# A hybrid decoder layer on one core: weight sums placed one unit before their split, both retention pairs in the other product order, one copy per value tile, later transposes and an earlier split

## The chip, the cores and the metric

One core of a Trainium2 chip runs the whole layer in one launch. The time is the device time of that launch in microseconds, as the median of several executions. The profile is taken of one further execution; its span is the time from the first to the last instruction that the profile shows.

## The reference

One layer on 512 tokens of width 1024, in float32. What is computed, cut to the lines that matter:

```python
h = rmsnorm(x, g_mix);  z = h @ w_in        # 9728 columns: retention q,k,v,gate; 3 attention groups; merge gates
y = retention_chunkwise(rq, rk, rv)          # 4 heads, chunks of 128
ret_branch = (silu(rg) * rmsnorm(y)) @ w_ret_out
for g, (window, dilation) in enumerate(((128, 1), (512, 4), (2048, 16))):
    o_g, lse_g = dilated_window_attention(aq[:, :, g], ak[:, :, g], av[:, :, g], window, dilation)
att_branch = (sum over g of softmax(lse)[g] * o_g) @ w_att_out
x = x + (gate_r * ret_branch + gate_a * att_branch) @ w_o
x = x + square(relu(rmsnorm(x, g_mlp) @ w_up)) @ w_down          # inner width 4096
return x + sigmoid(rmsnorm(x, g_ple) @ w_ple_gate) * (p @ w_ple_proj)
```

## The kernel before

**Three passes.** Every float32 product is made of three passes on PE (the tensor engine): the high part of one factor by the high part of the other, and two cross terms (`mm3`, lines 262 to 264). So each weight tile must be split in two. A weight unit is 256 rows by 512 columns, 512 KB. SP issues its load into a tile `raw` (`fetch`, line 212), ACT copies it, rounded, into `whi` (line 250), and DVE subtracts to get `wlo` (line 251). `units` keeps the splits two units ahead of PE, three in the last part (`AHEAD`). The pool has six `raw` tiles and four pairs of split tiles.

**Seven products.** Most large products are written as seven products of blocks in place of eight (`seven_products`). Product m takes one factor of the weights: B11, B21 and B22 are blocks as they are loaded; T1, T2, T3 and T4 are sums of blocks. Each is two units (0 and 1). For products that name T1 in `vector`, T1's sum is one DVE instruction of 128x1024 (line 226), which adds the raw tile of B11 into the raw tile of T1. It is written into the program right after the split of the unit in whose place `added` holds it: B11's own. The other sums come from DMAs on the queue of POOL which add in flight (lines 214 and 228).

The order of the products is a table of (product, half). With `SEVEN` the weight units run B11_0, T1_0, B11_1, T1_1, B21_0, and so on; with `HALVES` they run B11_0, B11_1, T1_0, T1_1, B21_0, ... `HALVES` is used for w_up and w_down (four products of each), `SEVEN` for the values of attention groups 1 and 2 and for the retention pairs (values and gates together, two products).

**Order on the engines.** A scheduler orders the instructions of ACT, DVE and PE except in stretches under `manual_schedule` (first attention part, w_o, and from the last w_down on), where ACT and DVE run in the order in which the code is written. What is put off runs through `later(lag, fn)`: `fn` runs after so many ticks, a tick being one panel of matmuls.

**The attention places.** `values_seven` evaluates the values of groups 1 and 2; products 6 and 7 give a tile `m` of 128 tokens, which SP copies into the strided value tile `v` with four DMAs of 32x512 each (line 764). `scores` has the exponentials `se` of a group turned by PE (`pe`, line 694) some ticks after the softmax. `rescale` makes the last merge factors: DVE f (line 863), ACT's exponential of f (864), DVE w, st, inv, f (866 to 871), ACT scales the sixteen blocks of `se` by inv (876), DVE copies f into `wide` (878), and PE transposes wide into `pc` (884).

**w_up.** `up_products` squares the rectified result, forms sums of it, and splits them as left factors of w_down. What is put into `before` runs inside the following w_down product at the index given; the split for product 2 stands at indexes 0 and 5 there (line 1340).

Of the kernel before, what the change touches and what calls it, by code (L numbers as in the profile page):

```python
# [17 lines left out]
P = 128  # L18
# [9 lines left out]
DIL = 4  # L28
# [47 lines left out]
def R(ap):  # L76
    return ap.bitcast(F32R)


class Block:  # L80
# [90 lines left out]
    def plan_seven(self, w, r0, c1, c2, order, vector=()):  # L171

        cols = (c1, c2)
        q = lambda i, j, u: w[r0 + 512 * i + 256 * u : r0 + 512 * i + 256 * (u + 1), cols[j] : cols[j] + 512]
        n = len(self.plan)
        units = [(FACTOR[m], v) for m, u in order for v in ((0, 1) if u is None else (u,))]
        at = lambda name, u: n + units.index((name, u))
        for name, u in units:
            if name == "T1":
                src = q(0, 1, u) if name in vector else (q(0, 1, u), q(0, 0, u))  # L180
                if name in vector:
                    self.added[at("B11", u)] = at("T1", u), at("B11", u)
            elif name == "T4" and name in vector:
                self.added[max(at("B21", u), at("T2", u))] = at("T2", u), at("B21", u)
                src = (None, at("T2", u))
            elif name[0] == "B":
                src = q(int(name[1]) - 1, int(name[2]) - 1, u)
            else:
                prev, ij = {"T2": ("T1", (1, 1)), "T3": ("B22", (0, 1)), "T4": ("T2", (1, 0))}[name]
                k = at(prev, u)  # L190
                self.chained[k] = q(*ij, u)
                src = (None, k)
            self.plan.append((src, None))
# [538 lines left out]
    def values_seven(self, scale, ready=None):  # L732

        nc = self.nc
        for j in range(2):
            self.force(("S", j))
        held, out = {}, {}

        def tile(n):
            if n not in out:  # L740
                out[n] = self.big("v")
            return out[n]

        def after(m, p, ps):
            t = p if m in (1, 2, 3, 6) else 2 + p
            main = m in (1, 2, 4)
            r = scale[0 if main else 1]
            by = {} if r is None else dict(scale=r[:, t : t + 1])
            if main:
                o = tile(0)[:, t]  # L750
            elif m in (3, 5):
                o = self.tmp("m3") if m == 3 else self.tabp.tile([P, 512], F32, tag="tab", name=self.nm("m5"))
                held[{3: 6, 5: 7}[m], p] = o
            else:
                o = held.pop((m, p))
            if m in (1, 3, 5, 4):
                nc.scalar.activation(o, ps, AF.Copy, **by)
            elif r is None:
                nc.vector.tensor_tensor(o, o, ps, op=ALU.add)
            else:  # L760
                nc.vector.scalar_tensor_tensor(o, ps, r[:, t : t + 1], o, op0=ALU.mult, op1=ALU.add)
            if m in (6, 7):
                for q in range(DIL):
                    nc.sync.dma_start(tile(1)[32 * t : 32 * (t + 1), q], o[q : P : DIL])
            if m in (2, 4) and ready is not None:
                ready(t, o)

        self.seven_products(self.left, after)
        return tile(0), tile(1)

    def scores(self, g, qT, kT, rq, past, held=None, lag=2):

        nc = self.nc
# [5 lines left out]
        def block(r):  # L779
# [17 lines left out]
                    hs = slice(2 * hp, 2 * hp + 2)  # L797
                    es.append(self.softmax(sc, 256, 2, self.mask[:, 0:256], rq[:, r, hs], m[:, hs], l[:, hs]))
            for e in es:
                self.later((5, 8, 11)[g], lambda e=e: turn(e, r), ("pT", g, r))  # L800

        def turn(e, r):
            if g == 2:
# [209 lines left out]
    def retention(self, dec, kd):  # L1013
# [8 lines left out]
        for pr in range(2):  # L1022
# [19 lines left out]
                    nc.scalar.activation(s, g, AF.Sigmoid, scale=r)  # L1042
                    nc.vector.scalar_tensor_tensor(g, g, r, s, op0=ALU.mult, op1=ALU.mult)

            self.seven_products(left, after)
            A.append(self.big("A"))
            for hh in range(2):
                self.ret_head(2 * pr + hh, (qT, kT, kd), tile("v"), tile("G"), inner, eps, A)
# [259 lines left out]
    def up_products(self, h2):  # L1308

        nc = self.nc  # L1310
        U, split = self.slots()
        held, before = {}, {}
        v = lambda ap: ap.rearrange("p (k t) -> p k t", k=2)

        def after(m, p, ps):
# [10 lines left out]
                nc.scalar.activation(x, x, AF.Relu, scale=1.0 if m == 2 else -1.0)  # L1326
            nc.scalar.activation(x, x, AF.Square)
            a11, a12, a21 = held.get((3, p)), held[1, p], held[5, p]
            if m == 6:
                split(1, v(a11), k)  # L1330
            elif m == 7:
                nc.vector.tensor_tensor(a11, a11, a21, op=ALU.subtract)
            elif m == 4:
                nc.vector.tensor_tensor(a21, x, a21, op=ALU.subtract)
                split(5, v(a21), k)
                self.differ(a21, x, a11)
                s3 = self.tmp("r3")
                rest = lambda m, a: lambda: split(m, v(a), k)
                third = lambda: self.differ(s3, a12, a21)
                for i, fn in ((p, third), (5 * p, rest(2, a12)), (1 + p, rest(3, s3)), (4 + p, rest(6, a21)),  # L1340
                              (7 + p, rest(7, a11)), (9 + p, rest(4, x))):
                    before.setdefault(i, []).append(fn)

        self.seven_products(lambda m, kk: (R(h2[m][:, 0, kk]), R(h2[m][:, 1, kk])), after, HALVES, "cb")
        return U, before


# [109 lines left out]
    def make_plan(self):  # L1457
# [7 lines left out]
        for c in range(2):  # L1465
            self.plan_cols(w, RQ + 256 * c, KD)
        for c in (0, 512):
            self.plan_seven(w, 0, RV + c, RG + c, SEVEN, ("T1", "T4"))
        self.plan_mix()
        self.plan_seven(a["w_o"][0], 0, 512, 0, SEVEN)  # L1470
        for half in range(2):
# [45 lines left out]
```

## Time and profile before

| what | us |
|---|---|
| median of 3 runs (lowest, highest) | 954.35 (953.08, 955.14) |
| the profiled execution, its own time | 955.36 |
| its span | 953.6 |
| PE busy | 943.3 |
| DVE busy | 718.4 |
| ACT busy | 562.1 |
| mean granted clock of PE, as a share of full speed | 0.997 |

The profiled execution took 1.01 us more than the median, and 1.8 us more than its span, which lies before the first and after the last instruction shown. PE's share of the span is 99%: a change gains either by making PE do less, or by closing the few places where it waits or runs at a lower clock. DVE and ACT are busy for 75% and 59% of the span; what they do counts only where PE waits for it.

### The profile page before, as it was taken

What the parts mean: (1) busy time and instruction counts of PE and PEld (TensorE: products, weight loads), DVE (VectorE), ACT (ScalarE), POOL (GpSimd) and SP (SyncE); (2) the same over time, 40 slices, a digit from 0 to 9 for tenths busy, and PEclk for the clock granted to TensorE, in tenths of its full rate; (3) what the DMA queues carried; (4) which work ended last, traced back from release to release, by engine and by line L of the source; (5) the groups of instructions that cost most, each with busy time, mean ns of one, the idle gap of its engine ahead of it and who ended that gap; (6) DMA issues with size and microseconds to landing.
All of it is one profiled execution on the core that took longest, in us unless ns stands there. A gap on an engine that the chain in (4) does not pass through costs nothing.

```text
span 953.6 us, 14325 instructions
## 1 busy us (share of the span) xinstructions
PE 943.3 (99%) x5357; PEld 826.2 (87%) x5357; DVE 718.4 (75%) x997; ACT 562.1 (59%) x1065; POOL 159.5 (17%) x140
## 2 busy tenths in 40 slices
PE   9999999999899999999999999999999999999998
PEld 6888888888788888999988888988998998998887
DVE  7789964766697849386937889799499689769953
ACT  5657775445745566576714446884494486467651
POOL 0322210222001112223012211111212302112100
PEclk9999999999999999999999999999999999999999
DMA  9953466258437645869737677868958968876911
GB/s 333 282 170 82 106 141 215 64 118 195 148 111 155 173 100 138 163 181 217 232 115 236 148 178 214 206 153 222 199 156 202 191 183 157 224 172 159 288 50 56
DMA packets 92549, 162.87 MB, mean 171 GB/s; under 512 B 8608, under 2 KB 20544, under 8 KB 92480
## 3 DMA queue, kind: packets, MB, share of 16 engines
q1 hardware_dynamic: 65168, 113.37, 36.4%
q0 software_dynamic: 23936, 46.14, 29.0%
q10 hardware_dynamic: 3376, 2.44, 0.9%
q8 instruction: 42, 0.69, 0.3%
q14 instruction: 27, 0.22, 0.1%
HBM read 153.49 MB, written 6.34 MB: 168 GB/s over the span
## 4 chain that ended last, share of the span: by engine, by line
PE 92%; DVE 3%; ACT 1%; issue 1%; DMA 1%; POOL 1%; SPq 0%; ACTq 0%; POOLq 0%; DVEq 0%
PE pg L264 25%; PE pg L262 25%; PE pg L263 25%; PE pa L264 3%; PE pa L263 3%; PE pa L262 3%; PE po L835 1%; PE ph L590 1%; DVE wlo L251 1%; PE pe L694 1%; PE sc L787 1%; PE ry L1083 1%; PE kv L1070 1%; PE ry L1085 1%; DVE ro L578 0%
## 5 line engine op out<-in xcount | busy, mean ns | idle before, releaser
L251 DVE TENSOR_TENSOR wlo<-raw,whi 128x1024 fp32r<-128x1024 f32 (+1 forms) x258 | 306.8, 1198 | 112.7 <-ACT whi L250 111.8
L250 ACT ACTIVATE whi<-raw 128x1024 fp32r<-128x1024 f32 (+1 forms) x257 | 266.3, 1041 | 212.1 <-PE pg L264 87.2
L263 PE MATMUL pg<-f,whi 128*128 128x256 f32 x384 | 108.7, 283 | 0.0
L264 PE MATMUL pg<-f,wlo 128*128 128x256 f32 x384 | 108.7, 283 | 0.0
L262 PE MATMUL pg<-f,whi 128*128 128x256 f32 x384 | 108.7, 283 | 0.0
L262 PE MATMUL pg<-whi,hh 128*128 128x512 f32 x248 | 98.6, 398 | 0.0
L264 PE MATMUL pg<-whi,hl 128*128 128x512 f32 x248 | 97.1, 392 | 0.0
L263 PE MATMUL pg<-wlo,hh 128*128 128x512 f32 x248 | 96.8, 390 | 0.0
L262 PE MATMUL pg<-whi,f 128*128 128x512 f32 x192 | 75.4, 393 | 0.0
L263 PE MATMUL pg<-wlo,f 128*128 128x512 f32 x192 | 74.8, 389 | 0.0
L264 PE MATMUL pg<-whi,f 128*128 128x512 f32 x192 | 74.8, 389 | 0.0
L262 PEld LDWEIGHTS pg<-f,whi 128*128 128x128 f32 x384 | 73.7, 192 | 0.2
L263 PEld LDWEIGHTS pg<-f,whi 128*128 128x128 f32 x384 | 73.7, 192 | 0.2
L264 PEld LDWEIGHTS pg<-f,wlo 128*128 128x128 f32 x384 | 73.7, 192 | 0.0
L228 POOL DMA_DIRECT2D raw<-in_w_in x32 | 38.9, 1216 | 197.8 <-DVE wlo L251 193.0
L264 PEld LDWEIGHTS pg<-whi,hl 128*128 128x128 f32 x248 | 46.6, 188 | 9.8
L263 PEld LDWEIGHTS pg<-wlo,hh 128*128 128x128 f32 x248 | 46.6, 188 | 9.2
L262 PEld LDWEIGHTS pg<-whi,hh 128*128 128x128 f32 x248 | 46.6, 188 | 9.2
L228 POOL DMA_DIRECT2D raw<-in_w_down x24 | 29.0, 1215 | 139.3 <-DVE wlo L251 108.2
L262 PE MATMUL pg<-whi,us 128*128 128x512 f32 x128 | 52.1, 407 | 0.0
L228 POOL DMA_DIRECT2D raw<-in_w_up x24 | 29.0, 1211 | 135.0 <-DVE wlo L251 124.7
L264 PE MATMUL pg<-whi,us 128*128 128x512 f32 x128 | 50.0, 391 | 0.0
(280 smaller groups left out, 2298.0 us busy)
## 6 DMA issues: line engine op xcount, KB each, us to landing
raw<-in_w_in SPq DMA_DIRECT2D x72, 512.0 KB, 4.1
raw<-in_w_in POOLq DMA_DIRECT2D x32, 512.0 KB, 6.2
raw<-in_w_up SPq DMA_DIRECT2D x32, 512.0 KB, 4.6
raw<-in_w_down SPq DMA_DIRECT2D x32, 512.0 KB, 4.6
raw<-in_w_up POOLq DMA_DIRECT2D x24, 512.0 KB, 6.6
raw<-in_w_down POOLq DMA_DIRECT2D x24, 512.0 KB, 5.9
x<-in_x SPq DMA_DIRECT2D x8, 512.0 KB, 8.2
raw<-in_w_ret_out SPq DMA_DIRECT2D x8, 512.0 KB, 3.8
```

Source lines behind the costliest of these rows:

```text
L228: self.nc.gpsimd.dma_start(raw, self.chained[i].rearrange("(k p) n -> p k n", p=P), accum_op=ALU.add)
L250: self.pin(nc.scalar.activation(R(hi[:, i]), raw[:, i], AF.Copy))
L251: nc.vector.tensor_tensor(R(lo[:, i]), raw[:, i], hi[:, i], op=ALU.subtract)
L262: t.matmul(ps, sh, mh, start=first, stop=False, skip_group_check=more)
L263: t.matmul(ps, sh, ml, start=False, stop=False, skip_group_check=more)
L264: t.matmul(ps, sl, mh, start=False, stop=last, skip_group_check=more)
L590: self.nc.tensor.transpose(ps[:, t * P : (t + 1) * P], rots[t][:, h * HD : (h + 1) * HD], self.ident)
L694: self.nc.tensor.transpose(ps[:, k * P : (k + 1) * P], e[:, k * P : (k + 1) * P], self.ident)
L787: nc.tensor.matmul(sc[:, h * P : (h + 1) * P], qT[:, h, rs], kT[:, h, rs], start=True, stop=True)
L835: nc.tensor.matmul(po[:, h * P : (h + 1) * P], v[:, vt, h * HD : (h + 1) * HD], pt, start=b == 0, stop=b == len(blocks) - 1)
L1070: nc.tensor.matmul(ps, kd[:, n, hs], v[:, n, c], start=True, stop=True)
L1083: nc.tensor.matmul(y, sT[0][:, r], v[:, i, c], start=True, stop=i == 0)
```

## The change

There are five edits.

1. In `plan_seven` T1's sum on DVE is put behind the split of the unit just before T1's own, in place of behind B11's. With `SEVEN` these are the same place; with `HALVES` the sum is written one unit later.
2. In `values_seven` one DMA of 32x4x512 (256 KB) takes the place of four of 32x512 (64 KB), for each of eight value tiles.
3. In `scores` the transposes of group 2's exponentials are put off by 15 ticks in place of 11.
4. The two retention pairs use `HALVES` in place of `SEVEN`, in the plan of the loads and in the products.
5. In `up_products` the split for product 2, for both halves p, runs at index 11 of the same w_up product (before its last unit), in place of at indexes 0 and 5 of the w_down product behind it.

```diff
--- before.py
+++ after.py
@@ -179,7 +179,7 @@
             if name == "T1":
                 src = q(0, 1, u) if name in vector else (q(0, 1, u), q(0, 0, u))
                 if name in vector:
-                    self.added[at("B11", u)] = at("T1", u), at("B11", u)
+                    self.added[at("T1", u) - 1] = at("T1", u), at("B11", u)
             elif name == "T4" and name in vector:
                 self.added[max(at("B21", u), at("T2", u))] = at("T2", u), at("B21", u)
                 src = (None, at("T2", u))
@@ -760,8 +760,7 @@
             else:
                 nc.vector.scalar_tensor_tensor(o, ps, r[:, t : t + 1], o, op0=ALU.mult, op1=ALU.add)
             if m in (6, 7):
-                for q in range(DIL):
-                    nc.sync.dma_start(tile(1)[32 * t : 32 * (t + 1), q], o[q : P : DIL])
+                nc.sync.dma_start(tile(1)[32 * t : 32 * (t + 1)], o)
             if m in (2, 4) and ready is not None:
                 ready(t, o)
 
@@ -797,7 +796,7 @@
                     hs = slice(2 * hp, 2 * hp + 2)
                     es.append(self.softmax(sc, 256, 2, self.mask[:, 0:256], rq[:, r, hs], m[:, hs], l[:, hs]))
             for e in es:
-                self.later((5, 8, 11)[g], lambda e=e: turn(e, r), ("pT", g, r))
+                self.later((5, 8, 15)[g], lambda e=e: turn(e, r), ("pT", g, r))
 
         def turn(e, r):
             if g == 2:
@@ -1042,7 +1041,7 @@
                     nc.scalar.activation(s, g, AF.Sigmoid, scale=r)
                     nc.vector.scalar_tensor_tensor(g, g, r, s, op0=ALU.mult, op1=ALU.mult)
 
-            self.seven_products(left, after)
+            self.seven_products(left, after, HALVES)
             A.append(self.big("A"))
             for hh in range(2):
                 self.ret_head(2 * pr + hh, (qT, kT, kd), tile("v"), tile("G"), inner, eps, A)
@@ -1309,7 +1308,7 @@
 
         nc = self.nc
         U, split = self.slots()
-        held, before = {}, {}
+        held, before, own = {}, {}, {}
         v = lambda ap: ap.rearrange("p (k t) -> p k t", k=2)
 
         def after(m, p, ps):
@@ -1326,7 +1325,9 @@
                 nc.scalar.activation(x, x, AF.Relu, scale=1.0 if m == 2 else -1.0)
             nc.scalar.activation(x, x, AF.Square)
             a11, a12, a21 = held.get((3, p)), held[1, p], held[5, p]
-            if m == 6:
+            if m == 2:
+                own.setdefault(11, []).append(lambda: split(2, v(x), k))
+            elif m == 6:
                 split(1, v(a11), k)
             elif m == 7:
                 nc.vector.tensor_tensor(a11, a11, a21, op=ALU.subtract)
@@ -1337,11 +1338,11 @@
                 s3 = self.tmp("r3")
                 rest = lambda m, a: lambda: split(m, v(a), k)
                 third = lambda: self.differ(s3, a12, a21)
-                for i, fn in ((p, third), (5 * p, rest(2, a12)), (1 + p, rest(3, s3)), (4 + p, rest(6, a21)),
+                for i, fn in ((p, third), (1 + p, rest(3, s3)), (4 + p, rest(6, a21)),
                               (7 + p, rest(7, a11)), (9 + p, rest(4, x))):
                     before.setdefault(i, []).append(fn)
 
-        self.seven_products(lambda m, kk: (R(h2[m][:, 0, kk]), R(h2[m][:, 1, kk])), after, HALVES, "cb")
+        self.seven_products(lambda m, kk: (R(h2[m][:, 0, kk]), R(h2[m][:, 1, kk])), after, HALVES, "cb", own)
         return U, before
 
 
@@ -1465,7 +1466,7 @@
         for c in range(2):
             self.plan_cols(w, RQ + 256 * c, KD)
         for c in (0, 512):
-            self.plan_seven(w, 0, RV + c, RG + c, SEVEN, ("T1", "T4"))
+            self.plan_seven(w, 0, RV + c, RG + c, HALVES, ("T1", "T4"))
         self.plan_mix()
         self.plan_seven(a["w_o"][0], 0, 512, 0, SEVEN)
         for half in range(2):
```

What this makes of the order, at three places. First DVE around the last merge factors of the attention (f to wide), with the retention's first T1 sum (`raw<-raw,raw`); before:

```order
L251 TENSOR_TENSOR wlo_2564<-raw_2561,whi_2563 128x1024
L863 TENSOR_TENSOR f_2484<-st_2159,st_1123 128x16
L226 TENSOR_TENSOR raw_2755<-raw_2755,raw_2749 128x1024
L866 TENSOR_TENSOR w_2487<-f_2484,st_1123 128x16
L867 TENSOR_TENSOR st_2159<-st_2159,w_2487 128x4x4
L870 RECIPROCAL inv_2490<-st_2159 128x16
L871 TENSOR_TENSOR f_2484<-f_2484,inv_2490 128x16
L878 COPY wide_2509<-f_2484 128x4x4
```

and now:

```order
L251 TENSOR_TENSOR wlo_2540<-raw_2537,whi_2539 128x1024
L862 TENSOR_TENSOR f_2463<-st_2147,st_1123 128x16
L865 TENSOR_TENSOR w_2466<-f_2463,st_1123 128x16
L866 TENSOR_TENSOR st_2147<-st_2147,w_2466 128x4x4
L869 RECIPROCAL inv_2469<-st_2147 128x16
L870 TENSOR_TENSOR f_2463<-f_2463,inv_2469 128x16
L877 COPY wide_2488<-f_2463 128x4x4
L226 TENSOR_TENSOR raw_2719<-raw_2719,raw_2707 128x1024
```

The sum has moved from behind f to behind wide. Second PE behind the transpose of wide (`pc`), at the start of the retention's query columns; `pe` are the transposes of the exponentials `se`. Before:

```order
L884 MATMUL pc_2551<-ident,wide_2509 16x128
L264 MATMUL pg_2179<-whi_2463,hl_148 128x512
L694 MATMUL pe_2598<-ident,se_2356 128x128 x2
L262 MATMUL pg_2616<-hh_145,whi_2557 128x512
L694 MATMUL pe_2598<-ident,se_2356 128x128 x2
L263 MATMUL pg_2616<-hl_147,whi_2557 128x512
L694 MATMUL pe_2605<-ident,se_2372 128x128
L264 MATMUL pg_2616<-hh_145,wlo_2558 128x512
L694 MATMUL pe_2605<-ident,se_2372 128x128
L262 MATMUL pg_2616<-hh_145,whi_2557 128x512
L694 MATMUL pe_2605<-ident,se_2372 128x128 x2
```

and now:

```order
L883 MATMUL pc_2527<-ident,wide_2488 16x128
L264 MATMUL pg_2167<-whi_2445,hl_148 128x512
L262 MATMUL pg_2578<-hh_145,whi_2533 128x512
L263 MATMUL pg_2578<-hl_147,whi_2533 128x512
L264 MATMUL pg_2578<-hh_145,wlo_2534 128x512
L262 MATMUL pg_2578<-hh_145,whi_2533 128x512
```

with the first `pe` of this group 24 matmuls of the query columns later:

```order
L263 MATMUL pg_2578<-hl_148,whi_2539 128x512
L264 MATMUL pg_2578<-hh_146,wlo_2540 128x512
L694 MATMUL pe_2633<-ident,se_2344 128x128 x4
L694 MATMUL pe_2640<-ident,se_2360 128x128 x4
L262 MATMUL pg_2579<-hh_145,whi_2533 128x512
```

The transposes, which stood between the first matmuls behind pc, follow the whole of the first unit's product. Third DVE in the last w_down, around the split of its two T1 units (`wlo` of the raw tiles that the sum writes); before:

```order
L251 TENSOR_TENSOR wlo_8448<-raw_8362,whi_8447 128x1024
L1301 TENSOR_TENSOR f_8400<-r_8090,f_8400 128x512
L251 TENSOR_TENSOR wlo_8453<-raw_8369,whi_8452 128x1024
L1306 SCALAR_TENSOR_TENSOR r_8090<-r_8429,r_8185 128x512
L1301 TENSOR_TENSOR f_8471<-r_8404,f_8471 128x512
L1306 SCALAR_TENSOR_TENSOR r_8436<-r_8025,r_8090 128x512
L251 TENSOR_TENSOR wlo_8478<-raw_8475,whi_8477 128x1024
```

and now:

```order
L251 TENSOR_TENSOR wlo_8423<-raw_8347,whi_8422 128x1024
L1300 TENSOR_TENSOR f_8378<-r_8066,f_8378 128x512
L226 TENSOR_TENSOR raw_8426<-raw_8426,raw_8341 128x1024
L1305 SCALAR_TENSOR_TENSOR r_8066<-r_8407,r_8161 128x512
L251 TENSOR_TENSOR wlo_8431<-raw_8426,whi_8430 128x1024
L1300 TENSOR_TENSOR f_8449<-r_8382,f_8449 128x512
L1305 SCALAR_TENSOR_TENSOR r_8414<-r_8001,r_8066 128x512
L251 TENSOR_TENSOR wlo_8456<-raw_8453,whi_8455 128x1024
```

The sum of the second T1 unit, which stood in the w_up product ahead, is now the second instruction ahead of that unit's wlo, and ACT's whi of the same tile stands between the two.

## Rows read from the trace of the kernel before

**Rows 1.** The page, busy time of each engine over the span, and the chain of waits by engine

```profile
PE 943.3 (99%) x5357; PEld 826.2 (87%) x5357; DVE 718.4 (75%) x997; ACT 562.1 (59%) x1065; POOL 159.5 (17%) x140
...
PE 92%; DVE 3%; ACT 1%; issue 1%; DMA 1%; POOL 1%; SPq 0%; ACTq 0%; POOLq 0%; DVEq 0%
```

**Rows 2.** Waits of PE: line waited for, us in total, times, longest

```profile
PE pc L884 <- DVE wide L878: 3.0, 1, 3.0
```

**Rows 3.** Timeline of SP, 244 to 264 us: start, duration, engine, line, operation

```profile
246.87 7.26 SPq L764 DMA_DIRECT2D v<-m  x8
```

**Rows 4.** Timeline of all engines, 250 to 257 us

```profile
250.78 0.17 DVE L863 TENSOR_TENSOR f<-st,st 128x16 f32<-128x16 f32 x1
...
251.69 0.20 ACT L864 ACTIVATE f<-f 128x16 f32<-128x16 f32 x1
...
252.70 0.39 PE L263 MATMUL pg<-wlo,hh 128*128 128x512 f32 x1
253.73 1.22 DVE L226 TENSOR_TENSOR raw<-raw,raw 128x1024 f32<-128x1024 f32 x1 [2.79 <-DMA v<-m]
...
254.88 0.17 DVE L866 TENSOR_TENSOR w<-f,st 128x16 f32<-128x16 f32 x1
...
255.78 0.18 DVE L878 COPY wide<-f 128x16 f32<-128x16 f32 x1
...
256.11 0.37 PE L884 MATMUL pc<-ident,wide 128*16 128x128 f32 x1 [3.02 <-DVE wide L878]
```

**Rows 5.** Windows: busy us of each engine, granted clock, DMA share

```profile
core 0: us, PE busy (x) PEld busy (x) DVE busy (x) ACT busy (x) POOL busy (x), PEclk, DMA share, GB/s
108.00:112.00 4.00, 3.17 (x14) 2.36 (x13) 3.93 (x8) 2.69 (x11) 1.71 (x2) 1.00 0.73 109
252.00:256.00 4.00, 1.09 (x5) 0.56 (x3) 2.09 (x6) 1.14 (x5) 0.00 (x0) 0.99 0.26 77
256.00:260.00 4.00, 3.89 (x16) 3.09 (x17) 0.00 (x0) 4.00 (x15) 0.00 (x0) 0.59 0.64 244
260.00:264.00 4.00, 4.00 (x23) 3.35 (x22) 3.26 (x6) 3.98 (x11) 0.00 (x0) 1.00 0.10 35
```

**Rows 6.** Timeline of ACT, 250 to 262 us

```profile
255.63 4.79 ACT L876 ACTIVATE se<-se,inv 128x128 f32<-128x128 f32 x16 [2.86 <-DVE inv L870]
```

**Rows 7.** Every instruction of line 226 (ns min/median/max)

```profile
L226 DVE TENSOR_TENSOR raw<-raw,raw x32: 1214/1218/1227, 56.9 to 854.8; 128x1024 f32<-128x1024 f32 x32
```

**Rows 8.** Timeline of DVE in the last w_down

```profile
867.80 0.68 DVE L1301 TENSOR_TENSOR f<-r,f 128x512 fp32r<-128x512 f32 x1
868.40 1.22 DVE L251 TENSOR_TENSOR wlo<-raw,whi 128x1024 fp32r<-128x1024 f32 x1
...
877.45 1.22 DVE L251 TENSOR_TENSOR wlo<-raw,whi 128x1024 fp32r<-128x1024 f32 x1
```

**Rows 9.** Timeline of PE in the last w_down

```profile
870.89 0.39 PE L262 MATMUL pg<-whi,f 128*128 128x512 f32 x1
...
871.34 0.39 PE L264 MATMUL pg<-whi,f 128*128 128x512 f32 x1
...
879.45 0.39 PE L263 MATMUL pg<-wlo,f 128*128 128x512 f32 x1
```

**Rows 10.** Windows again, in the last w_down

```profile
866.00:870.00 4.00, 4.00 (x20) 3.30 (x19) 4.00 (x6) 2.88 (x4) 1.20 (x1) 1.00 0.00 0
```

**Rows 11.** Timeline, first w_down, the second T1 weight unit on ACT, DVE and PE

```profile
628.46 1.05 ACT L250 ACTIVATE whi<-raw 128x1024 fp32r<-128x1024 f32 x1
...
630.04 1.22 DVE L251 TENSOR_TENSOR wlo<-raw,whi 128x1024 fp32r<-128x1024 f32 x1
...
635.37 0.39 PE L262 MATMUL pg<-whi,f 128*128 128x512 f32 x1
```

**Rows 12.** DMA issues: kind, count, KB each, median us to landing

```profile
v<-m SPq DMA_DIRECT2D x32, 64.0 KB, 4.2
```

**Rows 13.** Timeline of PE, 256 to 275 us, the first product with group-two values

```profile
269.76 1.05 PE L835 MATMUL po<-pT,v 128*128 128x128 f32 x8
```

## The prediction

> **What bounds the kernel now.** I read the page first: PE is busy for 943.3 of 953.6 us and 92% of the chain that ended last is PE [rows 1]. None of the five edits takes a matmul away, so work saved on DVE, ACT or SP is worth nothing in itself; only a place where PE waits or runs slowly can give time. The waits of PE name one such place of any size: 3.0 us, once, for `wide` [rows 2]. The timeline there shows why [rows 4]. PE starts its last matmul at 252.70 and the transpose of wide at 256.11. DVE had f at 250.78 and ACT its exponential from 251.69 to 251.89, but DVE, in order, stood before w at the retention's first T1 sum. That could not start before its load had landed, behind SP's eight copies of value tiles [rows 3], ran from 253.73 for 1.22 us, and only then came w at 254.88 and wide at 255.78.
>
> The windows show a second cost [rows 5]. PE was busy for 1.09 us of 252 to 256; in the next 4 us the granted clock was 0.59 of full speed, a mixture of the two levels 1.2 and 2.4 GHz, and from 260 on it was 1.00. So that window lost 4.00 x (1 - 0.59) = 1.6 us. A shorter pause cost no clock: in 108 to 112 PE was idle for 0.83 us and the grant stayed at 1.00. Stall and clock together: 4.5 us.
>
> **Edits 1 and 4 at the attention's end: -2.9 and -1.6.** The order now has the sum behind wide. The chain from w to the end of wide took 255.96 - 254.88 = 1.08 us [rows 4]. Started after the exponential, at some 251.95, it ends at 253.03. The transpose followed wide's end by 0.15 us, which gives 253.18 in place of 256.11: 2.9 us gained, with 0.25 us of idle left behind the matmul that ended near 252.93. That is less than the 0.83 us that cost no clock, so I take the 1.6 us as gained too. Bounds: stall 0 (if something else holds w) to 3.0 (the whole wait); clock 0 to 1.6. The sum itself is late now: it runs when its load lands, as before at 253.73, and its split is needed only after the query columns, so it costs nothing there.
>
> [...]
>
> **Edit 3: 0.** The first eight transposes `pe` leave the first matmuls behind pc and come 24 and more matmuls later, by 24 x 0.23 = 5.5 us (matmul starts of rows 9 give the 0.23: two steps in 0.45). ACT's sixteen scalings of `se` take 4.79 us [rows 6]. They can begin with inv near 252.8, as the chain above moves by 2.9 us, and end near 257.6, ahead of the transposes at 253.2 + 5.5 = 258.7. Without this edit PE would follow the scalings closely. Behind the transposes the first product with group two's values is at 269.76 [rows 13], 11 us later, which covers the delay. Bounds: 0, and a wait of at most one scaling, 0.3 us (4.79/16).
>
> **Edit 2: 0.** SP issues 8 DMAs for 32; the old ones took 7.26/8 = 0.9 us each on its queue [rows 3], so some 22 us of SP's time go. A 64 KB copy landed 4.2 us after issue [rows 12]. The last landed before 256 and the first matmul that reads them is at 269.76 [rows 13]; 14 us of cover hold even if one large copy takes three times as long. The loads of `raw` behind them may land sooner, but edit 1 has taken the sum that waited there out of PE's way. Bounds: 0 and 0, with the cover gone at most 4.2 us.
>
> **Edit 1 in w_up and w_down: 0 but for the last.** A sum one unit later, with the split behind it, can delay a T1 unit by 1.22 [rows 7] and ACT's copy, 1.05. In the first w_down the second T1 unit has whi done at 629.51 and wlo at 631.26, and PE takes it at 635.37 [rows 11]: 4.1 us to spare against 2.3. The w_up products and the retention pairs are written the same way.
>
> **Edit 1 in the last w_down: +0.9.** There DVE and ACT run as written, and DVE is full: 4.00 of 4.00 us [rows 10]. Its second T1 sum now stands between two splits. On before's clock: f ends at 868.48 [rows 8], the sum in the place of the old wlo runs 868.40 to 869.62, ACT's whi, which needs it, ends near 870.75 (1.05 and a hand-over), and wlo runs 870.75 to 871.97. PE takes two matmuls by whi of this unit first in the changed order and needs wlo at 871.34 [rows 9]: PE stands for 0.6 us. DVE is then later by 871.97 - 869.62 = 2.35 us; one instruction of 0.7 now lies inside the wait for whi, so 1.65 us remain for what is queued behind, which is every later split and every update of the residual. The unit with least to spare there has wlo done at 878.67 and is needed at 879.45 [rows 8, 9], 0.78 us. So PE is late by 1.65 - 0.78 = 0.9 us in all, the first 0.6 within it. Bounds: 0 (edit 5 takes one f of 0.68 out of this stretch, and DVE may come to it earlier) and 1.7 (no slack).
>
> **Edit 5: 0.** Two ACT copies and two DVE subtractions of 0.68 [rows 8] a product move a place earlier. PE has no wait in w_up or w_down [rows 2]; the cover is the slack of 4 us [rows 11]. With it gone they would cost 0.7 us for each of four products, 2.8.
>
> **The sum.** 955.36 (profiled execution) - 2.9 - 1.6 + 0.9 = 951.8. This execution stands 1.0 us above the median of the runs shown, 954.35, whose spread is 2.06; I take off half, and forecast **951.3 us**. A measurement of this kernel can tell about 0.2%, 1.9 us, from no change; 952.4 is the border.
>
> **The rivals.**
>
> *No new wait in the last w_down* (chance 0.17). For it: two f come out of the full stretch, and every edge is below 1 us. Against: an instruction of 1.22 us enters a DVE that is full. Time: 951.3 - 0.9 = 950.4.
>
> *The clock term isn't gained* (0.14), because the median holds little of it, or since the residual idle still lowers the grant. For it: it was seen once, in one profile. Against: 0.83 us of idle kept full clock. Time: 951.3 + 1.6 = 952.9. [...]
>
> *The change doesn't do what it says at wide* (0.08). The order has the sum behind wide, but w might be held by something that the old sum hid, such as a later exponential (ACT is busy with softmax until 251.69). Then the 4.5 us stay and the new wait comes on top: 955.36 + 0.9 - 0.5 = 955.8, within 0.2%.
>
> *Slower: the later sum is exposed in every product with `HALVES`* (0.05). Ten products now place a sum between its load and its split. If the split's lead over PE fell below the 2.3 us of sum and copy, each product would put a sum of 1.22 us on PE's path: 950.4 + 10 x 1.22 = 962.6. For it: in the last w_down it does so. Against: 4.1 us of lead in the first [rows 11]. It decides from a lead of 2.3 us down.
>
> **How the numbers follow.** The forecast has 0.50, the other 0.06 is for things I have not seen, of either sign. Faster by over 0.2% come the forecast (nine tenths of it), the first rival and little else, with a share of the unseen: 0.68. Within 0.2% lie the clock rival, the third and the forecast's upper edge: 0.24. Slower: 0.08. The range takes in the forecast with its bounds (no new wait and half the correction to the median at the lower end, the clock rival with 0.5 us at the upper): 949.5 to 953.4.
>
> **What would show it.** Right: no wait of PE for wide above 0.3 us, full clock in the 4 us behind it, sixteen scalings of se some 3 us earlier, a PE wait for whi or wlo of 0.6 to 0.9 us near 868 (all of it 4.5 us earlier), eight value copies of 256 KB. Wrong: a grant near 0.5 behind pc, a wait of PE for `se` or for a w_up split, or a wait in the last w_down above 2 us, which could take the clock with it.

## The result, and the profile after

The changed kernel took 958.11 us, the median of 6 runs (956.67 to 960.42), against 953.72 for the kernel before beside it (6 runs, 952.18 to 955.14): a ratio of 1.0052, with an interval of 1.0035 to 1.0069. So it is slower by some 5 us (3.3 to 6.6 by the interval), where 951.3 was forecast with a range up to 953.4. Its profiled execution took 960.42 us with a span of 958.6.

The gain at wide is there. The timeline of the changed kernel at that place, all engines (start, duration, engine, line, operation):

```profile
250.06 0.17 DVE L862 TENSOR_TENSOR f<-st,st 128x16 f32<-128x16 f32 x1
...
250.97 0.20 ACT L863 ACTIVATE f<-f 128x16 f32<-128x16 f32 x1
...
251.20 0.18 DVE L865 TENSOR_TENSOR w<-f,st 128x16 f32<-128x16 f32 x1 [0.98 <-ACT f L863]
...
251.98 0.39 PE L263 MATMUL pg<-wlo,hh 128*128 128x512 f32 x1
252.12 0.18 DVE L877 COPY wide<-f 128x16 f32<-128x16 f32 x1
...
252.45 0.27 PE L883 MATMUL pc<-ident,wide 128*16 128x128 f32 x1
```

DVE goes from f to wide with nothing but the wait for the exponential in between (0.98 us before w), and PE's transpose comes right behind its last matmul: 252.45, where [rows 4] had 256.11. From the start of f to the transpose it is 2.39 us, where those rows have 5.33: 2.9 us less than in that execution, as forecast. The windows behind it keep full clock (columns as in [rows 5]):

```profile
252.00:256.00 4.00, 3.92 (x18) 2.96 (x17) 0.27 (x2) 4.00 (x15) 0.00 (x0) 1.00 0.97 236
256.00:260.00 4.00, 4.00 (x23) 3.42 (x22) 2.94 (x5) 4.00 (x12) 0.00 (x0) 1.00 0.12 45
```

But PE now waits in places where it did not. The lists of PE's waits here and below (total, times, longest) leave out one of 1.4 us at the very start, which every kernel has, and most of those of 0.3 us and less. In the first profile of before only two others are longer than 0.3 us, the one of [rows 2] and 0.8 us for sc. In the changed kernel:

```profile
PE pg L262 <- DVE x L1285: 3.0, 2, 2.3
...
PE pg L262 <- ACT pp L533: 1.4, 1, 1.4
PE pg L262 <- DVE r L1324: 1.0, 2, 0.8
PE pt L380 <- DVE x L1285: 0.8, 1, 0.8
PE sc L794 <- DVE sm L678: 0.6, 1, 0.6
PE pg L263 <- DVE wlo L251: 0.5, 1, 0.5
PE pg L262 <- ACT whi L250: 0.5, 1, 0.5
PE pg L262 <- DVE ro L1005: 0.4, 1, 0.4
```

and before, for pp:

```profile
PE pg L262 <- ACT pp L533: 0.2, 1, 0.2
```

Three groups are new: x, the residual update at the end of w_down that frees a bank of PSUM for the next product; pp and pt at the beginning of w_up; and wlo and whi in the last w_down. Together they are some 6 us, where before had 0.2 of them. The wait for r at the end of w_up isn't new: the first profile of before has none, a second one (below) has 1.0 us. That for ro is (0.4 us); the changed kernel without edit 1 has none.

### The profile page after: what moved, and what is told of

The parts are those of the page before. It is cut to its first block, busy times and chain, and to the rows that moved or that the text cites. A ratio compares the mean times of both kernels' runs of the same rounds, so it can differ in the third digit from the quotient of the medians.

```text
span 958.6 us, 14293 instructions
## 1 busy us (share of the span) xinstructions
PE 943.9 (98%) x5357; PEld 824.9 (86%) x5357; DVE 718.9 (75%) x997; ACT 561.5 (59%) x1065; POOL 159.5 (17%) x140
## 4 chain that ended last, share of the span: by engine, by line
PE 73%; DVE 12%; ACT 6%; DMA 6%; issue 3%; POOL 1%; ACTq 0%; SPq 0%; DVEq 0%; POOLq 0%
PE pg L262 20%; PE pg L263 20%; PE pg L264 20%; DVE wlo L251 3%; DMA raw<-in_w_down 3%; PE pa L263 2%; PE pa L262 2%; PE pa L264 2%; ACT whi L250 2%; DVE f L1300 1%; DMA raw<-in_w_up 1%; DMA raw<-in_w_in 1%; PE po L834 1%; ACT r L1325 1%; PE ph L590 1%
## 5 line engine op out<-in xcount | busy, mean ns | idle before, releaser
L262 PE MATMUL pg<-whi,us 128*128 128x512 f32 x128 | 52.0, 407 | 0.4 <-DVE ro L1005 0.4
L226 DVE TENSOR_TENSOR raw<-raw,raw 128x1024 f32<-128x1024 f32 x32 | 38.9, 1221 | 17.8 <-DMA raw<-in_w_in 10.4
```

Source lines behind the costliest of these rows:

```text
L226: self.nc.vector.tensor_tensor(total, total, part, op=ALU.add)
L262: t.matmul(ps, sh, mh, start=first, stop=False, skip_group_check=more)
```

## The experiments

Each edit is that of the list in the section on the change. Lines are as in the kernel before, shifted by some in kernels that add lines.

### One edit at a time

Edit 4 alone:

```diff
-            self.seven_products(left, after)
+            self.seven_products(left, after, HALVES)
...
-            self.plan_seven(w, 0, RV + c, RG + c, SEVEN, ("T1", "T4"))
+            self.plan_seven(w, 0, RV + c, RG + c, HALVES, ("T1", "T4"))
```

> The kernel before with edit 4 alone (both retention pairs in the order HALVES, the sum's key as before). Theory A (edit 4 alone moves the sum behind wide, edits 1 and 5 make the loss): the wait of PE for wide falls from 3.0 us to under 0.4 us, the clock behind it stays at 1.00, and the time is 3 to 4.5 us below before. Theory B (the gain needs edit 1 too, since the sum's key sets where it stands): wait for wide still near 3 us, time within 0.5 us of before. Theory C (the gain needs edit 3: PE would follow the scalings of se): wait for wide gone, but waits of PE for se of 1 to 2 us behind it, time 1 to 2.5 us below before.

Measured: 952.38 us against 952.92 before, ratio 0.9993 (0.9984 to 1.0001). There is no wait for wide in its profile and no wait for se: edit 4 by itself puts the sum behind wide, and edits 1 and 3 aren't needed for it. But the gain is 0.7 us, not 3 to 4.5, and the interval has room for none.

Edit 1 alone:

```diff
-                    self.added[at("B11", u)] = at("T1", u), at("B11", u)
+                    self.added[at("T1", u) - 1] = at("T1", u), at("B11", u)
```

> The kernel before with edit 1 alone. Theory A: it changes nothing at wide; it costs at the beginning of w_up, where the second T1 sum now stands before the split of the per-layer embedding (about 2.2 us: a wait of PE for x of 0.9 and for pp of 1.6 in place of 0.3), and in the last w_down (about 1.5 us); none at the borders of w_up and w_down for the first three blocks. Time 3 to 4 us above before. Theory B (the later sum is exposed in each of the eight w_up and w_down products): some 8 us above before, with waits at the borders. Theory C (harmless but for the last w_down, as forecast): 0.9 us above before.

Measured: 957.18, ratio 1.0045 (1.0032 to 1.0058), 4.3 us above before: theories B and C fall, and A was a little low. Waits of 1.4 us for pp, 0.8 for wlo and 0.6 for x in the last w_down, and 0.8 still for wide. One of 1.1 us stands at the end of the first w_up (620.90). There DVE's T1 sum of the first w_down, which edit 1 leaves in its place, waited 1.37 us for its load, where before's profile has 0.48.

Edit 5 alone:

```diff
+            if m == 2:
+                own.setdefault(11, []).append(lambda: split(2, v(x), k))
+            elif m == 6:
-            if m == 6:
...
-                for i, fn in ((p, third), (5 * p, rest(2, a12)), (1 + p, rest(3, s3)), (4 + p, rest(6, a21)),
+                for i, fn in ((p, third), (1 + p, rest(3, s3)), (4 + p, rest(6, a21)),
```

> The kernel before with edit 5 alone. Theory A: DVE's two subtractions for product 2, now at the end of w_up, stand ahead of the sums that free PE's banks there (waits for r of 0.3 to 0.9 us at the end of w_up), and at the end of w_down the scheduler puts both T1 sums ahead of the residual updates x (waits for x of 0.9 to 2.5 us). Time 3 to 6 us above before. Theory B and C (edit 5 is covered by the slack of the splits): time within 0.5 us of before, no waits for r or x.

Measured: 954.57, ratio 1.0018 (1.0007 to 1.0029), 1.7 us above before: less than theory A asked for, but not nothing. Waits for x of 1.0 and 0.2 us at the ends of two w_down products, and 0.3 for wlo in the last w_down. The wait for r at the end of w_up (0.9) proves nothing: the kernel before shows it too in its second profile, below.

Edits 2, 3 and 4 without 1 and 5 (the hunks of `values_seven`, `scores` and the retention):

```diff
-                for q in range(DIL):
-                    nc.sync.dma_start(tile(1)[32 * t : 32 * (t + 1), q], o[q : P : DIL])
+                nc.sync.dma_start(tile(1)[32 * t : 32 * (t + 1)], o)
...
-                self.later((5, 8, 11)[g], lambda e=e: turn(e, r), ("pT", g, r))
+                self.later((5, 8, 15)[g], lambda e=e: turn(e, r), ("pT", g, r))
```

> The changed kernel without edits 1 and 5, so edits 2, 3 and 4 on the kernel before. Theory A: all of the gain and none of the loss: no waits for x, r or pp beyond those of before, 4 to 4.5 us below before, so about 949.5. Theory B (edit 1 is needed for the gain): within 0.5 us of before. Theory C (edit 2 or 3 costs something by itself): between 951 and 953.5, more than the run with edit 4 alone.

Measured: 952.34, ratio 0.9991 (0.9982 to 0.9999). Theory A falls, and edits 2 and 3 add nothing that can be told to edit 4 alone. The parts add up: -0.09% (edits 2 to 4), +0.45% (edit 1), +0.18% (edit 5) make +0.54%, and the whole change measured +0.52%.

### Where the gain went, and where edit 1 costs

The kernel before once more, without an edit:

> The kernel before itself, unchanged, profiled once more. Theory D (the 3.0 us wait for wide and the low clock behind it were a draw of one execution, since the load in front of the sum lands at different times): the wait of PE for wide is about 0.7 to 1.0 us, as in the two runs that keep that order, and the clock behind it 1.00; the span is some 950 to 951.5. Theory E (the wait is a trait of this kernel that the edits 1 and 5 each happened to lessen): the wait is again near 3 us with a granted clock near 0.6 behind it.

Measured: 952.25 us, span 950.5. Its waits of PE:

```profile
PE pg L262 <- DVE r L1325: 1.0, 2, 0.6
PE sc L795 <- DVE sm L678: 0.7, 1, 0.7
PE pc L884 <- DVE wide L878: 0.7, 1, 0.7
```

The wait for wide is 0.7 us, not 3.0, with a clock of 1.00 behind it. Six runs of this study keep the old order at wide in their profiles, with waits of 0.7, 0.7, 0.8, 1.2, 1.3 and 2.0 us; the 3.0 of [rows 2] is the longest of seven. The one with 2.0 is the run with the later sum in the last product alone, and it has the low clock as well, 0.60 in 256 to 260:

```profile
PE pc L885 <- DVE wide L879: 2.0, 1, 2.0
```

```profile
256.00:260.00 4.00, 4.00 (x14) 3.10 (x14) 0.49 (x1) 4.00 (x14) 0.00 (x0) 0.60 0.47 181
```

The load of the tile that the sum adds into shows why. SP issues it at 244.9 to 245.7, ahead of the eight value copies [rows 3] and not behind them; the copies are issued while it is under way. From issue to landing it took, with the wait for wide beside it:

| profile | landing, us | wait for wide, us |
|---|---|---|
| before, first | 8.0 | 3.0 |
| edit 1 in the last w_down alone | 7.0 | 2.0 |
| edit 1 in the first w_up alone | 6.3 | 1.3 |
| edit 5, three w_up products held (below) | 6.2 | 1.2 |
| edit 1 alone | 5.8 | 0.8 |
| edit 5 alone | 5.7 | 0.7 |
| before, again | 5.7 | 0.7 |

The wait is the landing less 5.0 us in all seven, and the sum starts 0.1 us behind the landing each time. (For the two longest the trace names a value copy as the last to land, as in [rows 4], and for the other five the load itself.) So theory D holds: the load lands at another time in each execution, and the profile of before was an unlucky one. Two of the seven are the kernel before; the others keep its order at this place and differ elsewhere. Together they have a wait of 1.4 us on average, and a lowered clock in two of seven.

How often the clock falls is also in the 88 plain runs of the kernel before that stood beside the experiments. Its mean over a run is 0.997 and 0.998 in the two profiles with the dip. Twelve of the 88 have 0.998 or less, with a median of 955.7 us; the other 76 have 952.9. Where it fell in those twelve isn't recorded. Wide may not be the only place: one of the six runs of the changed kernel, whose two profiles have no wait there, has 0.997. None of the twelve is among the 29 runs beside which edits 4, 1, 5 and 2 to 4 were measured, so the 0.7 us of edit 4 is most likely a price without the clock.

Edit 1 in the first w_up product alone, and in the last w_down alone (in `plan_seven` the new place is taken only where `late` is set, which the plan sets before its call):

```diff
-                    self.added[at("B11", u)] = at("T1", u), at("B11", u)
+                    self.added[at("T1", u) - 1 if self.late else at("B11", u)] = at("T1", u), at("B11", u)
...
+            self.late = f == 0
             self.plan_seven(a["w_up"][0], 0, 1024 * f + 512, 1024 * f, HALVES, ("T1",))
+            self.late = False
```

> The kernel before with edit 1 in the first w_up product alone. Theory A (the second T1 sum, which now stands on DVE before the split of the per-layer embedding, waits there for its load, and all that follows it is late): a wait of PE for pp of 1.3 to 1.7 us in place of 0.2, one for x of up to 0.9; time 1.3 to 2.5 us above before. Theory B (that wait is made good later by the slack of the splits): within 0.5 us of before.

Measured: 955.25 against 953.18, ratio 1.0021 (1.0008 to 1.0035). In the kernel before DVE makes the embedding's split in one go:

```profile
569.11 1.28 DVE L524 TENSOR_TENSOR plo<-pl,ph 128x512 fp32r<-128x512 f32 x2
```

and in this run:

```profile
566.14 0.68 DVE L525 TENSOR_TENSOR plo<-pl,ph 128x512 fp32r<-128x512 f32 x1
567.04 1.22 DVE L227 TENSOR_TENSOR raw<-raw,raw 128x1024 f32<-128x1024 f32 x1 [0.22 <-DMA raw<-in_w_up]
568.18 0.68 DVE L525 TENSOR_TENSOR plo<-pl,ph 128x512 fp32r<-128x512 f32 x1
```

and its longest waits of PE:

```profile
PE pg L263 <- ACT pp L534: 1.4, 1, 1.4
PE pc L885 <- DVE wide L879: 1.3, 1, 1.3
PE pg L263 <- DVE r L1326: 1.1, 1, 1.1
```

The sum (line 227 here) stands between the two halves of the embedding's split and takes 1.22 us; all that is queued behind it is late by as much, down to ACT's copy of pp. The wait for pp is 1.4 us, in the changed kernel as here; before it was 0.2. So it is the sum's own length that pp shows. What the sum waits for its load comes on top: here 0.22 us, and PE has no wait for x there; in the changed kernel 1.01, and there PE waits 0.8 for x (the wait of pt) ahead of pp.

The other (`late` set for `f == NF // 2 - 1` before the call for w_down, and not for w_up):

> The kernel before with edit 1 in the last w_down product alone, where DVE runs in the written order. Theory A (sum, copy and subtraction in a row behind each other, and DVE full): waits of PE of 1.5 to 1.9 us together near 868 to 880, time 1.2 to 2 us above before. Theory C (as forecast): 0.9 us. If neither this nor the run with the first product alone costs, the loss of edit 1 lies in the six products between.

Measured: 955.81, ratio 1.0023 (1.0010 to 1.0037), so 2.2 us (1.0 to 3.5): theory A's 1.2 to 2 lies within the interval, theory C's 0.9 just below it. The timeline of the last w_down, DVE, ACT and PE:

```profile
868.15 1.22 DVE L227 TENSOR_TENSOR raw<-raw,raw 128x1024 f32<-128x1024 f32 x1
...
869.40 1.06 ACT L251 ACTIVATE whi<-raw 128x1024 fp32r<-128x1024 f32 x1 [2.24 <-DVE raw L227]
...
870.50 1.23 DVE L252 TENSOR_TENSOR wlo<-raw,whi 128x1024 fp32r<-128x1024 f32 x1 [0.52 <-ACT whi L251]
...
871.78 0.50 PE L264 MATMUL pg<-wlo,f 128*128 128x512 f32 x1 [0.62 <-DVE wlo L252]
...
877.03 1.40 DVE L1287 SCALAR_TENSOR_TENSOR x<-pg,f,x 128x512 f32<-128x512 f32 x2
...
877.93 0.47 PE L263 MATMUL pg<-whi,f 128*128 128x512 f32 x1 [0.62 <-DVE x L1287]
```

Sum (868.15), ACT's whi, which must wait for it (869.40), wlo (870.50), and PE's matmul by wlo at 871.78, 0.62 us late. DVE does not catch up, and at 877.93 PE waits another 0.62, this time not for a split: it needs a bank that DVE's update of x frees. The first and the last product together make +0.44%, and edit 1 alone +0.45%: the six between show no cost of their own, though these intervals would hide one of some 2 us. (`plan_mix`, line 1232, uses `HALVES` as well, for the two products of the merge gates. Edit 1 moves their sums too, so they are among what shows no cost.)

The changed kernel without edit 1:

> The changed kernel without edit 1. Theory A (losses of edits 1 and 5 add): 1.5 to 2 us above before, less the 0.6 us that edits 2 to 4 give, so 953.5 to 954.5 when before is at 952.9; the waits for r and x at the borders of w_up and w_down stay, those for pp and for wlo in the last w_down are gone. Theory F (the two edits make each other worse): below before by 0.5 us.

Measured: 954.40, ratio 1.0015 (1.0003 to 1.0027). The wait for pp is 0.2 us as before and that of pt is gone; those for x (0.9) remain, and the one for wlo in the last w_down (0.5) too, against theory A. There is none for r. Within the intervals the losses of 1 and 5 add; theory F falls.

### Holding the sum's place

Is it the order of the products, or the place that the scheduler gives the sum? In four kernels the sums of line 226 were held in the written order on DVE, T1's in every product and those of T4 with them:

```diff
-                self.nc.vector.tensor_tensor(total, total, part, op=ALU.add)
+                self.tc.keep_in_program_order(self.nc.vector.tensor_tensor(total, total, part, op=ALU.add))
```

> The kernel before with T1's sum held in the written order on DVE, so that the scheduler can't put it ahead of what the code has before it: it now stands behind wide, behind the updates of x at the end of w_down and behind r at the end of w_up. Theory A (what costs is where the scheduler puts the sum, whose load may not have landed, not the order of the products): no wait of PE for wide above 0.4 us, none for r at the ends of w_up above 0.3, time 1 to 2 us below before. Theory G (before's sums cost nothing on average, the later ones delay the T1 splits): within 0.5 us of before, or waits for whi or wlo of T1 units.

> Edit 5 alone, and T1's sum held in the written order. Theory A (edit 5 costs because the scheduler then puts both sums ahead of the updates of x): no waits for x at the ends of w_down; time at or below before, by 0 to 1.5 us, so at least 1.5 us below the run with edit 5 alone. What is left above the run sum_kept is what the split itself costs at the end of w_up and in the last w_down (wait for wlo of 0.3 to 0.7). Theory H (the two subtractions themselves cost): as the run with edit 5 alone, 1.7 us above before.

> Edit 1 alone, and T1's sum held in the written order. Theory A (in the first w_up the later sum costs since it is put ahead of the embedding's split and waits for its load there; in the last w_down since DVE is full in the written order): the waits for pp above 0.3 and for x near 572 are gone, those near 868 to 880 stay, time 1 to 2.2 us above before, or 0.2 to 1.2 us when it also has the gain of sum_kept. Theory B (a later sum costs in itself): as edit 1 alone, 4.2 us above before.

> Edits 2, 3 and 4, and T1's sum held in the written order: the version that should beat both kernels. Theory A: no wait for wide, r or x above 0.4 us; 1 to 2.5 us below before. If edits 2 to 4 gain only by moving the sum behind wide, it equals sum_kept within 0.5 us.

Measured against 952.89: 960.31 with the hold alone (ratio 1.0077, 1.0063 to 1.0091), 961.28 with edit 5 (1.0085, 1.0071 to 1.0099), 962.46 with edit 1 (1.0097, 1.0080 to 1.0114), 959.74 with edits 2 to 4 (1.0069, 1.0056 to 1.0081). All four of my totals were wrong. The waits for wide and r went, as theory A said, and so did the long wait for pp with edit 1. But the hold itself costs 7 us. Waits of PE with the hold alone:

```profile
PE sc L795 <- DVE sm L678: 1.7, 2, 1.5
...
PE pa L263 <- DVE wlo L251: 1.4, 3, 0.5
PE pa L262 <- ACT whi L250: 0.7, 2, 0.5
PE pg L262 <- ACT whi L250: 0.6, 1, 0.6
PE pg L262 <- DVE x L1286: 0.5, 1, 0.5
```

The sums that the scheduler had put earlier are now late, and with them the splits behind: pa waits for wlo in three w_down products and for whi in the retention and the last w_down, and the scores of the first attention group wait 1.5 us at once, where the two profiles of before had 0.8 and 0.7. The waits that are new make some 4 to 5 of the 7 us; the rest isn't located. A hold on all 32 sums can't tell what one of them does, so the next runs held few.

T1's sums held in the last three w_up products alone, with edit 5, and with edits 2 to 4:

```diff
+                    if self.hold:
+                        self.held_sums.add(at("B11", u))
...
+                if i in self.held_sums:
+                    self.tc.keep_in_program_order(add)
...
+            self.hold = f > 0
             self.plan_seven(a["w_up"][0], 0, 1024 * f + 512, 1024 * f, HALVES, ("T1",))
+            self.hold = False
```

> Edit 5 alone, with T1's sums of the last three w_up products (and of these alone) held in the written order: at the ends of w_down they stand behind the updates of x again. Theory A (edit 5 costs by the place that the scheduler then gives the two sums): waits for x at 735 and 815 fall from 1.15 and 0.37 us to some 0.5 in all; time 0.5 to 1.5 us below the run with edit 5 alone (954.6 when before is at 952.9). Theory H (the sums are no matter; the two subtractions and the DMAs in front of the last splits are): within 0.4 us of the run with edit 5 alone.

> Edits 2, 3 and 4, with T1's sums of the last three w_up products held in the written order: whether the hold alone costs or gives there. Theory A: nothing, within 0.5 us of the run with edits 2, 3 and 4, as their order without the hold has x ahead of the first sum already. Theory I (a later sum delays the split of T1): 0.5 to 1.5 us above that run, and then the hold hides a gain of the same size in own_split_up_kept.

Measured against 953.56: 953.29 with edit 5 (ratio 0.9995, 0.9985 to 1.0005), where edit 5 without the hold had 1.0018; and 952.10 with edits 2 to 4 (0.9982, 0.9968 to 0.9995), where they had 0.9991 without. The end of the second w_down on DVE, in the kernel before:

```profile
736.26 1.23 DVE L251 TENSOR_TENSOR wlo<-raw,whi 128x1024 fp32r<-128x1024 f32 x1 [1.20 <-ACT whi L250]
737.41 0.74 DVE L1286 SCALAR_TENSOR_TENSOR x<-pg,f,x 128x512 f32<-128x512 f32 x1
738.07 1.21 DVE L226 TENSOR_TENSOR raw<-raw,raw 128x1024 f32<-128x1024 f32 x1
```

with edit 5 alone, DVE and PE:

```profile
733.59 1.23 DVE L251 TENSOR_TENSOR wlo<-raw,whi 128x1024 fp32r<-128x1024 f32 x1 [1.20 <-ACT whi L250]
...
734.74 1.22 DVE L226 TENSOR_TENSOR raw<-raw,raw 128x1024 f32<-128x1024 f32 x1
...
735.87 0.74 DVE L1286 SCALAR_TENSOR_TENSOR x<-pg,f,x 128x512 f32<-128x512 f32 x1
...
736.76 0.47 PE L262 MATMUL pg<-whi,f 128*128 128x512 f32 x1 [0.99 <-DVE x L1286]
```

and DVE with the hold:

```profile
732.56 0.75 DVE L1292 SCALAR_TENSOR_TENSOR x<-pg,f,x 128x512 f32<-128x512 f32 x1 [0.33 <-PE pg L270]
735.01 1.23 DVE L257 TENSOR_TENSOR wlo<-raw,whi 128x1024 fp32r<-128x1024 f32 x1 [1.70 <-ACT whi L256]
736.15 0.74 DVE L1292 SCALAR_TENSOR_TENSOR x<-pg,f,x 128x512 f32<-128x512 f32 x1
736.81 1.21 DVE L230 TENSOR_TENSOR raw<-raw,raw 128x1024 f32<-128x1024 f32 x1
```

In the kernel before the update of x follows the split, then the sum. With edit 5 and without the hold the split waits as long for its whi (1.20 us), but the sum (734.74) comes next, and only then the update of x, for whose bank PE waits 0.99 us before the last of the seven products (736.76). With the hold x stands ahead of the split (732.56), the sum comes last, and no wait for x is left in the list. (The 1.15 and 0.37 us of the expectation are 0.99 and 0.21 in the list of waits of the run with edit 5 alone.) So edit 5's loss is the place that the scheduler gives the sums in the w_down from which edit 5 takes two subtractions; theory H falls. Why the scheduler chooses so is not shown. With edits 2 to 4 the hold costs nothing, so it hides no gain in the other run. It may itself give some of the 0.23% there, as the run with edits 2 to 4 is 0.09% lower with it than without, which is within the noise. That version has the lowest median of the study, clear of before but not of edits 2 to 4 without the hold, and its waits of PE are:

```profile
PE sc L800 <- DVE sm L684: 0.5, 1, 0.5
PE pg L268 <- DVE r L1330: 0.4, 1, 0.4
```

The changed kernel once more:

> The changed kernel itself, profiled once more. Theory A: the waits for pp (1.4 us) and near 572 come again to a tenth, since the order makes them; those at the ends of w_up and w_down are again there, but of other sizes, since they hang on when loads and accumulating DMAs land (0.3 to 2.5 us each); the wait in the last w_down is 1.3 to 1.9 us in all. No wait for wide above 0.4 us. Theory B (the waits at the ends of w_down were one draw): no wait for x above 0.4 us.

Measured: 960.65 us, span 958.9. Its waits:

```profile
PE pg L262 <- DVE x L1285: 1.7, 1, 1.7
...
PE pg L262 <- ACT pp L533: 1.4, 1, 1.4
...
PE pg L262 <- DVE r L1324: 0.6, 1, 0.6
PE pt L380 <- DVE x L1285: 0.6, 1, 0.6
PE pg L263 <- DVE wlo L251: 0.5, 1, 0.5
PE pg L262 <- ACT whi L250: 0.5, 1, 0.5
```

Against the first profile: pp 1.4 and 1.4, wlo 0.5 and 0.5, whi 0.5 and 0.5, which the order makes; x 3.0 and 1.7, r 1.0 and 0.6, pt 0.8 and 0.6, which don't come back. Two of the expectations failed: pt (near 572) was to come again to a tenth, and the last w_down was to have 1.3 to 1.9 us, where both profiles have 1.0. A landing stands at the head of the chain for x and for pt. Ahead of the wait of 1.7 ACT's whi for the last split waited 2.96 us for its raw tile to land, and split, sum and update of x follow in a row (817.01, 818.16, 819.29). Ahead of pt the sum waited 0.85 us for its load, and 1.01 in the first profile. For r it is not shown.

## Why the prediction was wrong, point by point

**What bounds the kernel, and the wait at wide.** The mechanism was right: the sum stood before w, edit 4's order takes it away, and the wait is gone. That the load came behind the eight copies was a misreading, since SP issued it ahead of them. The step that failed is the price. "2.9 us gained" and the clock's 1.6 were read from one execution as if each had them. Seven profiles of the same order have 0.7 to 3.0 us, 1.4 on average, and the low clock twice; edit 4 alone gained 0.7 us, 1.5 at most by its interval, in runs where before kept its clock. The sign was in the rows: the sum had waited 2.79 us for a DMA, and a wait that ends with a landing varies from run to run. The rival that the clock isn't gained went this way, but took away too little. The Trainium skill, "TensorE: Matmul & The Clock Gate", "What's actually happening", says of the start of a kernel that the count of slow matmuls differs between runs of one kernel and shouldn't be fitted. Here a dip in the middle of a kernel, which that sentence doesn't speak of, came in two of seven profiles of one order.

**Edit 1 at wide.** The forecast named it together with edit 4. It has no part in the gain: alone it leaves the order there as it was, since the retention then still has `SEVEN`, where both keys are the same place, and edit 4 alone is enough.

**Edit 1 in the first w_up, "0 but for the last".** Here a step failed in kind. I compared the lead of T1's own split (4.1 us) with the delay of the sum (2.3), and that part holds: no wait for a T1 split appears in the six products between. What I did not ask is who stands behind the sum on DVE. In the first w_up it is the embedding's split, and the cost is 2.0 us (0.8 to 3.3). I asked it for the last product alone.

**Edit 1 in the last w_down, +0.9.** Right in mechanism and place: sum, whi, wlo in a row, at 868.15, 869.40 and 870.50, and PE late by 0.6 us as worked out. Too small in the rest: I let DVE's lateness end at the slack of the tightest split, but an update of x, which frees PE's bank, came too late as well. The run with this alone cost 2.2 us (1.0 to 3.5), of which two waits of 0.6 us are seen; the rest isn't located.

**Edit 5, 0.** It failed. The cover named was the slack of the splits, and PE's only wait for a split in that run is 0.3 us, in the last w_down. The loss is that the scheduler, given a w_down with two subtractions fewer, put both T1 sums ahead of the updates of x. That is a move in the order outside the lines that the edit touches, 1.7 us (0.7 to 2.8).

**Edits 2 and 3, 0.** Right together, within the noise: with edit 4 they make 952.34, without them 952.38. They were not run apart from each other.

**The rivals.** The slower one named a sum exposed in all ten products and 962.6. It had the sign right, but not the mechanism: two of the products show a loss (twelve have `HALVES` in the changed kernel, with the two of the merge gates), and most of it comes from what stands behind the sums, not from T1. Its chance of 0.05 was far too low, since each place where a 1.22 us instruction moves on an engine in order was asked one question only.

**The sum over again.** The base of the forecast, 955.36 less 0.5, was 1.1 us above the 953.7 measured beside the change. The gain at wide was put 3.8 us too high, the last w_down 1.3 too low, and the first w_up and edit 5 stood at nothing for 2.0 and 1.7. With these 951.3 becomes 959.0, and 958.1 was measured, so what is left lies within the intervals.

## What to carry to other kernels

A wait that ends with a landing has no price in one profile: take a second execution, or put its whole spread, down to nothing, in the range. When an instruction moves on an engine that runs in order, ask of every place where it moves what now stands behind it, the updates that free PSUM banks first, and not only when its own result is due. Where a scheduler decides, compare the order of the whole engine: an edit that takes work out of one stretch can move another instruction ahead of the one that matters, and holding just that instruction in place (here, in three w_up products) gives the loss back, while holding all of them costs more than it gives.

## What the hardware showed

PE's clock fell behind the waits of 3.0 and 2.0 us at the same place (0.59 and 0.60 in the four microseconds behind) and not behind those of 0.7 to 1.3. Waits that end with a landing came out 1 to 2 us apart in executions of one order (wide 0.7 to 3.0; x 3.0 and 1.7); those that the order alone makes came back to 0.1 us. One load of 512 KB, issued just ahead of eight copies, landed 5.7 to 8.0 us later. Runs of one kernel beside each other spread by 0.7 to 5.8 us. In the 88 of the kernel before, those with the low clock stand at the upper end (955.7 against 952.9); that the landings make the rest of the spread was not tried.
